# Four products in the first pass over x, its loads cut and queued anew, ten warm-up matmuls for thirteen

## The chip, the cores and the metric

The kernel runs on one core of one Trainium2 chip. The metric is the device time of one execution in microseconds (us); lower is better. The engines named below are TensorE (PE in the profile, its weight loads PEld), VectorE (DVE), ScalarE (ACT), GpSimd (POOL) and SyncE (SP). Loads from HBM are issued by SP, ACT or POOL, each on a queue of its own: q1 is SP's, q10 ACT's, q0 POOL's.

## The reference, cut to what matters

It is one decoder layer over x of 512 tokens by 1024 columns in float32. The change lies in its first step, the gate and up products of the first feed-forward half; everything behind it stays as it is.

```python
x = x + 0.5 * swiglu(rms_norm(x, ffn1_norm), ffn1_gate, ffn1_up, ffn1_down)   # D_FF = 2816
h = rms_norm(x, mix_norm)
...                                   # gated recurrence, short convolution, cross-attention
x = x + 0.5 * swiglu(rms_norm(x, ffn2_norm), ffn2_gate, ffn2_up, ffn2_down)
return rms_norm(x, final_norm)
def swiglu(h, w_gate, w_up, w_down):
    return (jax.nn.silu(h @ w_gate) * (h @ w_up)) @ w_down
```

## The kernel before, in words

x lies transposed on the chip in `xall`: eight tiles k of 128 columns by 512 tokens (256 KB each). A product (m, j) is one block of 128 hidden columns of the gate (j = 0) or up (j = 1) weights: eight weight tiles of 128x128, 64 KB each, against the eight tiles of x, summed in one bank of PSUM. The kernel keeps float32 accuracy by splitting each operand into a high and a low part: `split_x` (lines 123 to 126) gives `x_f1…h` on ACT and `x_f1…l` on DVE, the `split` of `weight_steps` (lines 108 to 111) gives `whi` on ACT and `wlo` on DVE. `mm3` (lines 116 to 121) then makes three matmuls of 512 columns: high by high (L119), high by low (L120), low by high (L121). One product is 24 matmuls.

The order of the first feed-forward half is in `Half.run`. It begins with `first_tile` (lines 472 to 509), which is written by hand: three products, (0,0), (0,1) and (1,0), are made side by side, k by k, so that each tile of x is used three times as it arrives. Its weight pieces come in three cuts (k = 0; 1 and 2; 3 to 7), one unit on each of the three queues, and all of x on SP. Ahead of it thirteen float32 matmuls of 128 columns on a constant tile (line 71, two passes each in the trace) run while nothing has arrived yet. Behind it `run` makes (1,1), then sums the squares of x over the columns on TensorE (`norm.tokens`, `psn_f`), makes (2,0), spreads the row of scales by two matmuls (`norm.rows`, `psb_f`, line 169), and makes (2,1), (3,0) and (3,1). Only with that row (`rsb_f`, called `bc`) can DVE finish any of these products.

Weight units take turns in three buffers each of `raw`, `whi` and `wlo` in `wpool`; a fourth unit waits until the first is split (`raw`) and until its last matmul is done (`whi`, `wlo`). The pool `hp` of the half holds six buffers tagged `raw` and four each of `ah` and `al`, used later: `raw` for seven-product blocks (`Half.load`, lines 293 to 310), `ah` and `al` for the hidden tiles.

The order of instructions on each engine is set at build time by a scheduler from the order of the program and its own costs; at run time each engine takes them strictly in that order. A load issued by ACT stands in ACT's own stream.

Of the kernel before, what the change touches and what calls it, by code (L numbers as in the profile page):

```python
# [8 lines left out]
F32 = mybir.dt.float32  # L9
F32R = mybir.dt.float32r  # L10
# [5 lines left out]
P = 128  # L16
# [4 lines left out]
KT = D // P  # L21
# [17 lines left out]
def decoder_layer(ctx: ExitStack, tc: tile.TileContext, xT, memT, vecs, masks, ident_d,  # L39
                  w1, w1d, w_in, w_i, w_out, w_q, w_k, w_v, w_o, w2, w2d, gfin, out):  # L40
    nc = tc.nc
    const = ctx.enter_context(tc.tile_pool(name="const", bufs=1))
    xpool = ctx.enter_context(tc.tile_pool(name="xpool", bufs=KT))
    wpool = ctx.enter_context(tc.tile_pool(name="wpool", bufs=3))
# [4 lines left out]
    def bank(name):  # L49
        return psp.tile([P, 512], F32, tag="ps", name=name)  # L50

    def r32(ap):
        return ap.bitcast(F32)
# [13 lines left out]
    early = const.tile([P, 1], F32, name="early")  # L67
    nc.scalar.activation(early, mhalf[:, :1], AF.Silu)
    warm = bank("warm")
    for i in range(13):  # L70
        nc.tensor.matmul(warm[:, :P], lhsT=ones, rhs=ones, start=True, stop=True)

    vec = const.tile([P, V_LB], F32, name="vec")
# [6 lines left out]
    xall = xpool.tile([P, KT, S], F32, tag="x", name="xall", bufs=1)  # L80
    x = [xall[:, k] for k in range(KT)]
# [4 lines left out]
    def weights(src, shape):  # L86

        raw, hi, lo, load, split = weight_steps(src, shape)
        load(0, shape[0])
        split(0, shape[0])  # L90
        return hi, lo

    def weight_steps(src, shape):
        n = n_unit[0]
        n_unit[0] += 1
        raw = wpool.tile([P, 1024], F32, tag="raw", name=f"raw{n}")
        hi, lo = (wpool.tile([P, 1024], F32R, tag=t, name=f"{t}{n}") for t in ("whi", "wlo"))
        a, b = shape
        w = a * b

        def load(k0, k1, queue=nc.sync):
            c = slice(k0 * b, k1 * b)
            if len(src.shape) == 3:
                queue.dma_start(raw[:, c].rearrange("p (a b) -> p a b", a=src.shape[1]), src)
            else:
                queue.dma_start(raw[:, c], src[:, c])

        def split(k0, k1):
            c = slice(k0 * b, k1 * b)
            nc.scalar.activation(hi[:, c], raw[:, c], AF.Copy)  # L110
            nc.vector.tensor_tensor(lo[:, c], raw[:, c], r32(hi[:, c]), ALU.subtract)  # L111

        v = lambda t: t[:, :w].rearrange("p (a b) -> p a b", b=b)
        return raw, v(hi), v(lo), load, split

    def mm3(out, wh, wl, xh, xl, first, last):


        nc.tensor.matmul(out, lhsT=wh, rhs=xh, start=first, stop=False)  # L119
        nc.tensor.matmul(out, lhsT=wh, rhs=xl, start=False, stop=False)  # L120
        nc.tensor.matmul(out, lhsT=wl, rhs=xh, start=False, stop=last)  # L121

    def split_x(t, gcol, hi, lo):
        g = vec[:, gcol:gcol + 1]
        nc.scalar.activation(hi, t, AF.Copy, scale=g)
        nc.vector.scalar_tensor_tensor(lo, t, g, r32(hi), op0=ALU.mult, op1=ALU.subtract)
# [47 lines left out]
    def new_split(tag, pool, name, n=S, bufs=KT):  # L174
        return (pool.tile([P, n], F32R, tag=tag + "h", name=name + "h", bufs=bufs),
                pool.tile([P, n], F32R, tag=tag + "l", name=name + "l", bufs=bufs))
# [21 lines left out]
    class Half:  # L198
# [196 lines left out]
        def run(self, first, begin, down, fill, last):  # L395

            p0, p1 = first() if first else ([self.product(0, 0), self.product(0, 1)], [self.product(1, 0)])
            p1.append(self.product(1, 1))  # L400
            self.norm.tokens()
            p2 = [self.product(2, 0)]
            self.bc = self.norm.rows()
            p2.append(self.product(2, 1))
            steps, later = self.inputs_steps()
            self.finish(0, p0)
            self.finish(1, p1)
            steps.pop(0)()
            p3 = [self.product(3, 0), self.product(3, 1)]
            self.finish(2, p2)  # L410
            steps.pop(0)()
            begin(steps + later, lambda: self.finish(3, p3))
            before = None
            for m in range(CLASSIC, FT, 2):
                p1, p5, r6, p2, r7, p4, p3 = self.seven(m)
                p1()
                if before:
                    for s in before:
                        s()
                p5()  # L420
                r6()
                part = [q for q, (a, b) in enumerate(PARTS) if b == m and m > CLASSIC]
                if part:
                    down(part[0])
                p2()
                r7()
                before = p4, p3
            fill()
            for s in before:
                s()  # L430
            last()
# [38 lines left out]
    norm, xs, _ = prepare(V_FFN1, "f1")  # L470

    def first_tile():
        units = [weight_steps(w1[m, j], (KT, P)) for m, j in ((0, 0), (0, 1), (1, 0))]
        ps = [bank(f"ps_f1_{n}") for n in range(3)]
        queues = (nc.sync, nc.scalar, nc.gpsimd)

        def load(k0, k1):
            for u, queue in zip(units, queues):
                u[3](k0, k1, queue)

        nc.sync.dma_start(x[0], xT[:, 0])
        load(0, 1)
        nc.sync.dma_start(x[1], xT[:, 1])
        load(1, 3)
        nc.sync.dma_start(xall[:, 2:4], xT[:, 2:4])
        load(3, 8)
        nc.sync.dma_start(xall[:, 4:6], xT[:, 4:6])
        nc.sync.dma_start(xall[:, 6:8], xT[:, 6:8])
        cuts = [0, 1, 3, 8]
        for k0, k1 in zip(cuts, cuts[1:]):  # L490
            for k in range(k0, k1):
                hi, lo = new_split("x", xpool, f"x_f1{k}")
                split_x(x[k], V_FFN1 + k, hi, lo)
                xs.append((hi, lo))
                if k == k0:
                    for u in units:
                        u[4](k0, k1)
                for j in range(3):
                    mm3(ps[j], units[j][1][:, k], units[j][2][:, k], hi, lo, k == 0, k == KT - 1)
        for k in range(KT):  # L500
            norm.add(x[k])
        nc.scalar.dma_start(ident, ident_d)
        nc.scalar.dma_start(lbv, vecs[:, V_LB:V_LB + 8].rearrange("p (r h) -> p r h", r=2))
        for n in range(0, len(LEVELS), 4):
            e = min(n + 4, len(LEVELS))
            mskf = tmp.tile([P, 4, 2, 64], F32, tag="t2", name=f"mskf{n}")
            nc.scalar.dma_start(mskf[:, :e - n], masks[:, n:e])
            nc.vector.tensor_copy(msk[:, n:e], mskf[:, :e - n])
        return ps[:2], ps[2:]

    norm_m, xs_m, done_m = prepare(V_MIX, "mx")
    with tc.tile_pool(name="hid1", bufs=1, reuse_waits="tile") as hp:
        half = Half("f1", hp, xs, norm, w1, V_FFN1)
# [31 lines left out]
        def last1():  # L545
# [9 lines left out]
            for d in range(4, KT):  # L555
                down_tile(half, "f1", d, len(PARTS) - 1, src1)
                done_m(d)

        half.run(first_tile, begin1, down1, fill1, last1)


    norm_a, xs_a, done_a = prepare(V_XATT, "xa")
    with tc.tile_pool(name="mix", bufs=8, reuse_waits="tile") as mp:
        def big(name):
            return mp.tile([P, NH, S], F32, tag="b", name=name)
# [24 lines left out]
        f = big("f")  # L590
# [7 lines left out]
        for h in range(NH):  # L598
            p = pf[h]
            t = tmp.tile([P, S], F32, tag="t0", name=f"zf{h}")  # L600
# [4 lines left out]
        for h in range(NH):  # L605
            p = project(h)
            t = tmp.tile([P, S], F32, tag="t0", name=f"zq{h}")
# [89 lines left out]
        for hh in range(NH):  # L697
            ps = bank(f"ps_s0_{hh}")
# [14 lines left out]
        for li, h in enumerate(LEVELS):  # L713
# [7 lines left out]
            for half in range(2):  # L721
                ps = bank(f"ps_l{h}_{half}")
# [14 lines left out]
            for r in range(2):  # L737
                qv = qp[:, :, r].rearrange("p g (b u c) -> p g b u c", u=2, c=h)[:, :, :, 1 - r]
                kv = kp[:, :, r].rearrange("p g (b u c) -> p g b u c", u=2, c=h)[:, :, :, r]
                shape = [P, 2 * NH, nb, h]  # L740
# [9 lines left out]
        for half in range(2):  # L750
            ps = bank(f"ps_o1_{half}")
            for n in range(4):
                hh, i = 2 * half + n // 2, 2 * (n % 2)
# [12 lines left out]
        for hh in range(NH):  # L766
            ps = bank(f"ps_o2_{hh}")
# [16 lines left out]
        for i in range(TT):  # L784
            ps = bank(f"ps_o{i}")
# [17 lines left out]
        for hh in range(NH):  # L803
            ps = bank(f"ps_t{hh}")
            for i in range(TT):
                nc.tensor.transpose(ps[:, i * P:(i + 1) * P], on[i][:, hh], ident)
            t = tmp.tile([P, S], F32, tag="t0", name=f"yh{hh}")
            nc.vector.scalar_tensor_tensor(t, ps, vec[:, V_HG + hh:V_HG + hh + 1], sg[:, hh],
                                           op0=ALU.mult, op1=ALU.mult)
            hi, lo = new_split("y", mp, f"yh{hh}")  # L810
# [35 lines left out]
        for m in range(KT):  # L846
# [4 lines left out]
            t = tmp.tile([P, MEM], F32, tag="t0", name=f"km{m}")  # L851
# [129 lines left out]
    with tc.tile_pool(name="hid2", bufs=1, reuse_waits="tile") as hp:  # L981
        half = Half("f2", hp, xs_2, norm_2, w2, V_FFN2)
# [28 lines left out]
        def down(i, j, k, wh, wl):  # L1011
            c = slice(i * P, (i + 1) * P)
            a, b = half.hidden(k)
            p, h, l = po[i][j], wh[:, j], wl[:, j]
            nc.tensor.matmul(p, lhsT=a[:, c], rhs=h, start=k == L0, stop=False)
            nc.tensor.matmul(p, lhsT=a[:, c], rhs=l, start=False, stop=False)
            nc.tensor.matmul(p, lhsT=b[:, c], rhs=h, start=False, stop=k == FT - 1)
# [118 lines left out]
```

## Time and profile before

| what | value |
|---|---|
| median of three runs | 1113.97 us (1113.47 to 1115.74) |
| profiled execution, its own time | 1115.02 us |
| span in its trace, first to last instruction | 1113.2 us |
| PE busy | 1094.7 us (98% of the span) |
| DVE, ACT, POOL busy | 731.2, 485.9, 74.6 us |
| mean granted TensorE clock | 0.995 of full |

The profiled execution took 1.05 us more than the median, and 1.8 us of its time lies outside the span. Times in the rows count from the start of the span.

### The profile page before, as it was taken

The page shows a single profiled execution, that of the slowest core. Times are in us where ns is not written, and L with a number is a line of the kernel's source. Part 1 is how long each engine was busy: PE and PEld are TensorE (multiplying, and loading weights), DVE is VectorE, ACT ScalarE, POOL GpSimd, SP SyncE. Part 2 cuts the span into 40 slices and gives each one's busy share as a digit, 9 for nine tenths or more (in the row PEclk, how much of TensorE's full clock was granted, in tenths as well). Part 3 has the DMA queues.
Part 4 walks back from the last instruction along what each step waited for, and adds up shares of the span by engine and source line. Part 5 has one row for each costly group of instructions (what it writes and reads, how often), then busy time and mean ns, then how long its engine had stood idle before and what let it go on. Part 6 is the DMA issues. An engine that isn't in the chain of part 4 may idle for free. (4 is left out here: it accounts for less than half of the span.)

```text
span 1113.2 us, 15967 instructions
## 1 busy us (share of the span) xinstructions
PE 1094.7 (98%) x6528; PEld 979.4 (88%) x6528; DVE 731.2 (66%) x980; ACT 485.9 (44%) x667; POOL 74.6 (7%) x75
## 2 busy tenths in 40 slices
PE   9989999999999999999999999999989999999997
PEld 7869998998998888888889888888889989989995
DVE  6786755764768566885686556554987747755744
ACT  6435533542545344323364345342545524533553
POOL 0001100110100000000100000000011101100102
PEclk9999999999999999999999999999999999999999
DMA  6467764673523332222244324232287835764521
GB/s 210 127 177 172 195 143 125 164 194 116 160 45 110 97 100 80 81 76 85 67 120 138 122 77 133 74 96 78 84 230 190 186 109 137 203 146 135 114 76 76
DMA packets 68745, 140.53 MB, mean 126 GB/s; under 512 B 4944, under 2 KB 20560, under 8 KB 68672
## 3 DMA queue, kind: packets, MB, share of 16 engines
q1 hardware_dynamic: 54112, 108.02, 30.7%
q0 software_dynamic: 12544, 28.84, 13.2%
q10 hardware_dynamic: 2016, 2.66, 0.7%
q8 instruction: 51, 0.84, 0.3%
q14 instruction: 22, 0.18, 0.1%
HBM read 137.40 MB, written 2.10 MB: 125 GB/s over the span
## 5 line engine op out<-in xcount | busy, mean ns | idle before, releaser
L110 ACT ACTIVATE whi<-raw 128x1024 fp32r<-128x1024 f32 (+4 forms) x143 | 138.0, 970 | 329.5 <-issue 67.4
L111 DVE TENSOR_TENSOR wlo<-raw,whi 128x1024 fp32r<-128x1024 f32 (+4 forms) x143 | 158.6, 1112 | 83.7 <-ACT whi L110 83.1
L316 ACT ACTIVATE whi<-b_f 128x1024 fp32r<-128x1024 f32 x72 | 76.3, 1060 | 104.5 <-issue 34.3
L317 DVE TENSOR_TENSOR wlo<-b_f,whi 128x1024 fp32r<-128x1024 f32 x72 | 88.2, 1225 | 42.3 <-ACT whi L316 40.9
L120 PE MATMUL psd_f<-al_f,whi 128*128 128x512 f32 x280 | 109.1, 390 | 0.0
L121 PE MATMUL psd_f<-ah_f,wlo 128*128 128x512 f32 x280 | 109.1, 390 | 0.0
L119 PE MATMUL psd_f<-ah_f,whi 128*128 128x512 f32 x280 | 108.5, 390 | 0.0
L317 DVE TENSOR_TENSOR wlo<-t_f,whi 128x1024 fp32r<-128x1024 f32 x54 | 66.1, 1224 | 42.6 <-ACT whi L316 42.6
L192 DVE SCALAR_TENSOR_TENSOR xall<-psd_f,xall 128x512 f32<-128x512 f32 x52 | 35.4, 691 | 71.4 <-PE psd_f L121 71.4
L316 ACT ACTIVATE whi<-t_f 128x1024 fp32r<-128x1024 f32 x54 | 57.0, 1056 | 56.6 <-issue 21.3
L121 PEld LDWEIGHTS psd_f<-ah_f,wlo 128*128 128x128 f32 x280 | 52.6, 188 | 10.9
L119 PEld LDWEIGHTS psd_f<-ah_f,whi 128*128 128x128 f32 x280 | 52.6, 188 | 10.8
L120 PEld LDWEIGHTS psd_f<-al_f,whi 128*128 128x128 f32 x280 | 52.6, 188 | 10.7
L338 PE MATMUL psD_f<-q1h_f,whi 128*128 128x256 f32 x144 | 41.2, 286 | 8.3 <-ACT whi L316 8.3
L338 PE MATMUL psA_f<-a11h_f,wlo 128*128 128x256 f32 x144 | 42.2, 293 | 0.0
L338 PE MATMUL psA_f<-a11h_f,whi 128*128 128x256 f32 x144 | 42.1, 292 | 0.0
L338 PE MATMUL psA_f<-a11l_f,whi 128*128 128x256 f32 x144 | 42.1, 292 | 0.0
L338 PE MATMUL psD_f<-q1l_f,whi 128*128 128x256 f32 x144 | 41.0, 284 | 0.0
L338 PE MATMUL psA_f<-a22h_f,whi 128*128 128x256 f32 x144 | 40.9, 284 | 0.0
L338 PE MATMUL psD_f<-q4h_f,wlo 128*128 128x256 f32 x144 | 40.8, 284 | 0.0
L338 PE MATMUL psA_f<-n2h_f,wlo 128*128 128x256 f32 x144 | 40.8, 284 | 0.0
L338 PE MATMUL psA_f<-a22h_f,wlo 128*128 128x256 f32 x144 | 40.8, 284 | 0.0
(778 smaller groups left out, 3209.7 us busy)
## 6 DMA issues: line engine op xcount, KB each, us to landing
b_f<-in_w SPq DMA_DIRECT2D x54, 512.0 KB, 4.0
t_f<-in_w POOLq DMA_DIRECT2D x54, 512.0 KB, 5.7
raw<-in_w_in SPq DMA_DIRECT2D x24, 512.0 KB, 3.5
t_f<-in_w SPq DMA_DIRECT2D x18, 512.0 KB, 5.3
raw<-in_w1d SPq DMA_DIRECT2D x20, 384.0 KB, 3.1
raw<-in_w SPq DMA_DIRECT2D x13, 512.0 KB, 3.5
raw<-in_w2d SPq DMA_DIRECT2D x16, 384.0 KB, 3.1
raw<-in_w2d SPq DMA_DIRECT2D x10, 512.0 KB, 3.4
```

The costliest lines, as they stand in the source:

```text
L110: nc.scalar.activation(hi[:, c], raw[:, c], AF.Copy)
L111: nc.vector.tensor_tensor(lo[:, c], raw[:, c], r32(hi[:, c]), ALU.subtract)
L119: nc.tensor.matmul(out, lhsT=wh, rhs=xh, start=first, stop=False)
L120: nc.tensor.matmul(out, lhsT=wh, rhs=xl, start=False, stop=False)
L121: nc.tensor.matmul(out, lhsT=wl, rhs=xh, start=False, stop=last)
L192: nc.vector.scalar_tensor_tensor(x[k], ps, scale, x[k], op0=ALU.mult, op1=ALU.add)
L316: nc.scalar.activation(hi, raw, AF.Copy)
L317: nc.vector.tensor_tensor(lo, raw, r32(hi), ALU.subtract)
L338: nc.tensor.matmul(o, lhsT=a[:, i, w], rhs=b, start=first and i == 0 and k == 0 and n == 0, stop=k == 3 and n == 2, skip_group_check=True)
```

## The change

Ten warm-up matmuls run in place of thirteen. `first_tile` makes four products, (0,0), (0,1), (1,0) and (1,1); the fourth unit's three tiles are taken from `hp` (one buffer each of `raw`, `ah`, `al`), and `run` no longer makes (1,1) by itself. The cuts are now k = 0; 1; 2 and 3; 4 and 5; 6 and 7. In each cut x comes in two halves of 256 tokens. In the first three cuts SP loads one half of x and unit 0, ACT the other half and unit 1; in the last two SP loads all of these; POOL loads units 2 and 3 throughout. SP and ACT so issue 19 loads on top of `vec` where there were 11, POOL ten where there were three.

```diff
-    for i in range(13):
+    for i in range(10):
         nc.tensor.matmul(warm[:, :P], lhsT=ones, rhs=ones, start=True, stop=True)
...
-            p0, p1 = first() if first else ([self.product(0, 0), self.product(0, 1)], [self.product(1, 0)])
-            p1.append(self.product(1, 1))
+            p0, p1 = first() if first else ([self.product(m, j) for j in range(2)] for m in range(2))
             self.norm.tokens()
...
     def first_tile():
-        units = [weight_steps(w1[m, j], (KT, P)) for m, j in ((0, 0), (0, 1), (1, 0))]
-        ps = [bank(f"ps_f1_{n}") for n in range(3)]
-        queues = (nc.sync, nc.scalar, nc.gpsimd)
-
-        def load(k0, k1):
-            for u, queue in zip(units, queues):
+
+        spare = (half.hp.tile([P, 1024], F32, tag="raw", name="raw_f1x", bufs=6),
+                 half.hp.tile([P, 1024], F32R, tag="ah", name="whi_f1x", bufs=4),
+                 half.hp.tile([P, 1024], F32R, tag="al", name="wlo_f1x", bufs=4))
+        units = [weight_steps(w1[n // 2, n % 2], (KT, P), spare if n == 3 else None) for n in range(4)]
+        ps = [bank(f"ps_f1_{n}") for n in range(4)]
+        cuts = [0, 1, 2, 4, 6, 8]
+        steps = list(zip(cuts, cuts[1:]))
+        for k0, k1 in steps:
+
+            other = nc.scalar if k1 <= 4 else nc.sync
+            for queue, t in ((nc.sync, slice(0, 256)), (other, slice(256, 512))):
+                queue.dma_start(xall[:, k0:k1, t], xT[:, k0:k1, t])
+            for u, queue in zip(units, (nc.sync, other, nc.gpsimd, nc.gpsimd)):
                 u[3](k0, k1, queue)
-
-        nc.sync.dma_start(x[0], xT[:, 0])
-        load(0, 1)
-        nc.sync.dma_start(x[1], xT[:, 1])
-        load(1, 3)
-        nc.sync.dma_start(xall[:, 2:4], xT[:, 2:4])
-        load(3, 8)
-        nc.sync.dma_start(xall[:, 4:6], xT[:, 4:6])
-        nc.sync.dma_start(xall[:, 6:8], xT[:, 6:8])
-        cuts = [0, 1, 3, 8]
-        for k0, k1 in zip(cuts, cuts[1:]):
+        for k0, k1 in steps:
             for k in range(k0, k1):
...
-                for j in range(3):
+                for j in range(4):
                     mm3(ps[j], units[j][1][:, k], units[j][2][:, k], hi, lo, k == 0, k == KT - 1)
```

## Rows read from the trace of the kernel before

**Rows 1.** The page: busy time and share of the span, by engine.
```profile
PE 1094.7 (98%) x6528; PEld 979.4 (88%) x6528; DVE 731.2 (66%) x980; ACT 485.9 (44%) x667; POOL 74.6 (7%) x75
```

**Rows 2.** Timeline, PE, to 38 us: start, duration, line, tile, count, idle before, releaser.
```profile
1.09 5.67 PE L71 MATMUL warm<-ones 128*128 128x128 f32 x26 [1.09 <-DVE mhalf L61]
...
5.52 0.64 PE L71 MATMUL warm<-ones 128*128 128x128 f32 x2
6.37 0.39 PE L71 MATMUL warm<-ones 128*128 128x128 f32 x2
6.51 0.96 PE L119 MATMUL ps_f<-x_f10h,whi 128*128 128x512 f32 x3
8.47 0.39 PE L121 MATMUL ps_f<-x_f10h,wlo 128*128 128x512 f32 x1
9.67 0.50 PE L119 MATMUL ps_f<-x_f11h,whi 128*128 128x512 f32 x1 [0.81 <-ACT whi L110]
14.35 0.39 PE L119 MATMUL ps_f<-x_f13h,whi 128*128 128x512 f32 x1
24.33 0.39 PE L121 MATMUL ps_f<-x_f17h,wlo 128*128 128x512 f32 x1
25.46 0.51 PE L119 MATMUL ps_f<-x_f10h,whi 128*128 128x512 f32 x1 [0.74 <-ACT whi L110]
26.04 0.95 PE L147 MATMUL psn_f<-inv_d,acc_f 128*128 128x1 f32 x8
26.85 0.48 PE L119 MATMUL ps_f<-x_f10h,whi 128*128 128x512 f32 x1
37.38 0.63 PE L169 MATMUL psb_f<-dg_f,ones_r 128*128 128x512 f32 x2
```

**Rows 3.** Windows: length; busy PE, PEld, DVE, ACT, POOL; granted clock; DMA share; GB/s.
```profile
37.38:75.95 38.57, 38.57 (x171) 31.94 (x170) 36.95 (x57) 20.37 (x30) 1.28 (x1) 1.00 0.41 120
75.95:81.37 5.42, 0.40 (x3) 0.19 (x1) 3.00 (x6) 1.06 (x1) 0.77 (x1) 1.00 0.96 236
81.37:85.00 3.63, 3.63 (x17) 3.63 (x18) 2.43 (x2) 1.05 (x1) 1.20 (x1) 0.53 0.57 205
```

**Rows 4.** Timeline of ACT and DVE: first splits; table load; the last diagonal tile.
```profile
4.24 0.72 ACT L125 ACTIVATE x_f10h<-xall,vec 128x512 fp32r<-128x512 f32 x1 [1.56 <-DMA vec<-in_vecs]
4.87 0.49 ACT L110 ACTIVATE whi<-raw 128x128 fp32r<-128x128 f32 x2
6.52 0.31 ACT L110 ACTIVATE whi<-raw 128x128 fp32r<-128x128 f32 x1 [1.16 <-DMA raw<-in_w]
22.96 1.28 ACT L579 ACT_TABLE_LOAD   x1
30.54 0.69 DVE L161 TENSOR_TENSOR dg_f<-ident,rsl_f 128x512 fp32r<-128x512 f32 x1
```

**Rows 5.** Waits of SP's queue, 0 to 60 us: total us, times, longest.
```profile
SPq L488 <- DMA xall<-in_xT: 3.6, 1, 3.6
```

**Rows 6.** DMA issues, 0 to 30 us: count, KB each, median us to landing.
```profile
raw<-in_w POOLq DMA_DIRECT2D x1, 128.0 KB, 6.2
raw<-in_w SPq DMA_DIRECT2D x1, 64.0 KB, 2.9
raw<-in_w ACTq DMA_DIRECT2D x1, 64.0 KB, 3.0
raw<-in_w POOLq DMA_DIRECT2D x1, 64.0 KB, 5.2
```

**Rows 7.** Timeline of POOL: its first three loads (L106).
```profile
1.27 1.86 POOL L106 DMA_DIRECT2D raw<-in_w  x3 [0.83 <-POOLq L1122]
```

**Rows 8.** Waits of SP's queue, 25 to 110 us: total us, times, longest.
```profile
SPq L106 <- DVE wlo L111: 25.2, 4, 9.5
```

**Rows 9.** POOL's queue, 2.5 to 5.5 us, then 5.5 to 8.5: packets, MB, share.
```profile
q0 software_dynamic: 36, 0.09, 16.2%
...
q0 software_dynamic: 104, 0.37, 34.1%
```

More of the change, by code (lines that the diff above doesn't have):

```diff
@@ L91, in weights, with weight_steps @@
         return hi, lo
-    def weight_steps(src, shape):
+    def weight_steps(src, shape, tiles=None):
         n = n_unit[0]
         n_unit[0] += 1
-        raw = wpool.tile([P, 1024], F32, tag="raw", name=f"raw{n}")
-        hi, lo = (wpool.tile([P, 1024], F32R, tag=t, name=f"{t}{n}") for t in ("whi", "wlo"))
+        raw, hi, lo = tiles or (wpool.tile([P, 1024], F32R if t[0] == "w" else F32, tag=t, name=f"{t}{n}")
+                                for t in ("raw", "whi", "wlo"))
         a, b = shape
```

## Prediction, made before the changed kernel ran

> **What bounds the kernel now.** I read the page first: TensorE is busy 98% of the span and no other engine above 66% [rows 1]. So there is little to win but time in which TensorE stands still or runs at half clock, and the change touches only the first forty of 1113 us. Therefore the timeline of PE comes next [rows 2]. The reader is to see its holes. The warm-up passes fill 1.09 to 6.5 us. The first product's first matmuls start at 6.51, but the last one of the first cut starts at 8.47 and the next work at 9.67. The last matmul of the pass starts at 24.33, and only at 25.46 does (1,1) begin. `psb_f`, without which DVE can finish no product, starts at 37.38.
>
> Dense, a matmul of 512 columns takes 0.227 us: 45 of them start from 14.35 to 24.33, 44 steps in 9.98 us [rows 2]. Up to 37.38 TensorE needs 120 of them, 27.24 us, and 0.81 for `psn_f` (26.04 to 26.85). From 6.51 that would end at 34.56, so 2.8 us of holes lie between. With the late start at 6.51 this is all that the change can collect.
>
> What lies behind `psb_f` decides whether it may keep it, so the windows are read next. From 37.38 to 75.95 PE is busy the whole time and DVE 36.95 of 38.57 us; then PE stands for 5.02 us until the weight unit `t1` is there, and the granted clock is 0.53 for the 3.6 us after it [rows 3].
>
> **The warm-ups.** Thirteen make 26 passes, ten make 20. The passes start 0.21 us apart, the 21st at 5.52 [rows 2], so PE is free at 5.52 in place of 6.5. Their clock: two passes from 5.52 on take 0.64 us, two from 6.37 on 0.39 [rows 2]. TensorE thus ran at its lower level (1.2 GHz) nearly to 6.3 us and at 2.4 GHz after. The windows print 1.00 there; the spacing is what I trust. Real matmuls that start before 6.3 are slow: at the lower level 17 matmuls of 256 columns took 3.63 us [rows 3], so I take 0.427 us for one of 512.
>
> **The first cut (k = 0).** The first half product could have begun earlier before, too: `x_f10h` runs from 4.24 to 4.96 and the first two `whi` pieces from 4.87 [rows 4], so the operands of the first matmul are there at about 5.2. Now ACT also issues the other half of x, behind `vec`. An issue costs ACT some 0.4 us, and some of its loads wait: in the trace SP's last x load was held 3.6 us until an earlier x tile had landed [rows 5]. I take 5.7 for the first matmul, with 5.5 and 6.0 as bounds.
>
> There are now twelve matmuls for k = 0. From 5.7 to 6.3 one and a half run slowly, the other ten take 2.3 us: 8.6 if nothing is missing. But two of the four weight pieces come by POOL. A 64 KB piece landed 2.9 us after its issue on SP, 3.0 on ACT and 5.2 on POOL [rows 6], where it was issued at 1.27 [rows 7], so at 6.5. That is why the third `whi` waited until 6.52 [rows 4]. POOL's next 128 KB, issued about 0.6 later, took 6.2, so they landed at 8.0. Unit 3's first 64 KB are half of that: 7.3 by interpolation, and its `whi` is split at 7.6 (0.3 us [rows 4]). If the instruction order keeps all high-by-high matmuls first, as the three of before are at 6.51 [rows 2], nine matmuls stand behind that split: 7.6 + 2.0 = 9.6. If unit 3's come last, 8.6 stays. I take 9.1; landing as late as the 128 KB did (8.0) would make it 10.4.
>
> The Trainium skill (DMA: Bandwidth & Descriptors, Issuing engines are not separate DMA queues) says that loads from all three engines end up on the same 16 DMA engines and interleave there, and that spreading them saves only issue time. This trace differs for small pieces, 5.2 against 2.9 and 3.0 us; by the page unit 3 would not be late, and the cut would end at 8.6.
>
> **The other cuts.** Before, the x tile of k = 1 arrived behind other loads, and the hole from 8.7 to 9.67 came of it. Now its halves are issued ahead of the later cuts, and POOL's pieces for it are 64 KB each. Each k lasts 12 × 0.227 = 2.7 us on PE instead of 2.0, which gives all later cuts more time to arrive: the splits of one k cost ACT about 0.72 + 4 × 0.3 = 1.9 us at most [rows 4]. I count 84 × 0.227 = 19.1 us and 0.2 for short waits on `x_l`, with 0 and 1 as bounds. The pass ends at 9.1 + 19.1 + 0.2 = 28.4.
>
> **Behind the pass.** `psn_f` takes 0.8, (2,0) 24 × 0.227 = 5.45, slow starts 0.1: `psb_f` at 34.7. Before, the hole up to 25.46 came because ACT loaded a table at 22.96 [rows 4] just when it should have split (1,1). Now the unit to be split is (2,0), and nine matmuls of k = 7 and `psn_f` (2.8 us) cover it, as its buffers are released by unit 0, first of four. That is twice the table load (1.28), so it covers that too, or most of it with a split, if it falls there. If the cover fails, the price is about the 0.9 of before. The diagonal tiles for `psb_f` were ready at 31.2 [rows 4], 4.3 after `psn_f`; now 29.2 + 4.3 = 33.5, hidden by (2,0) with 1.2 to spare. The spare tiles of unit 3 shift the turns of `hp` by one: later tiles still wait for the same predecessors, one of them for the spare, free since 28.4. I cost that at nothing; if it failed, the x tiles of the blocks would wait for TensorE.
>
> **The sum.** 37.4 − 34.7 = 2.7 us. Does it last to the end? Up to 75.95 PE runs without a hole, so it keeps the lead. The 5 us wait hangs on a chain of loads on SP, which before that waits for DVE's splits of `wlo` [rows 8], and these for TensorE and for `rsb_f`. Nothing in it goes by absolute time, so I move all of it by 2.7. The profiled execution took 1115.0, 1113.2 of span and 1.8 around it that no edit touches; 1115.0 − 2.7 = 1112.3; against the median, which is 1.05 lower, **1111.3 us**.
>
> **The rivals.**
> *Dense:* unit 3's piece lands with the others and the first cut ends at 8.6, the waits are nil: pass 27.7, `psb_f` 34.0, gain 3.3, 1110.6 us. For it speaks that POOL's pieces are smaller now; against it the 5.2 us for 64 KB.
>
> *Unit 3 stalls the cut:* all high-by-high matmuls first and the landing at 8.0: 1.3 us later than my 9.1, gain 1.4, 1112.6 us. This is a gain too small to be told from none (I take 0.2%, 2.2 us, as the bound).
>
> *Late clock:* PE idles between 5.52 and the first product and again in the first cut; the clock then rises only with k = 1. Twelve matmuls at 0.427 from 5.7 end at 10.8, 1.7 late: gain 1.0, 1113.0 us. For it speaks that before it rose behind warm-up passes without a hole, from 1.09 to 6.3 [rows 2], which now end sooner. The Trainium skill (TensorE: Matmul & The Clock Gate, Part 1, What's actually happening) says that half rate is the default and that activity releases it; the two pass lengths agree with it.
>
> *Given back:* the wait at 81 us does not move along, or another order of instructions later costs as much: 1114.0 us. Against it stand the waits of SP's queue [rows 8].
>
> *Slower:* POOL's queue stays as slow as it was at first. It moved 0.09 MB from 2.5 to 5.5 us and 0.37 in the next three [rows 9]. At 0.03 MB/us the pieces of k = 1 (0.26 MB in all) are through at 11.2 and land about 12.9; PE reaches the end of k = 1 at 15.2, not 11.8, 3.4 late, and the pieces of the third cut are late again. If this holds to about 14 us, another 1.5 is lost there, and the 2.7 turn into a loss of 2.2: 1116.2 us. Below that it isn't slower. Against it: the queue's rate rose fourfold by itself once the first crowd of loads was through.
>
> **How the numbers follow.** Mine (gain 2.0 to 3.1) 0.40, of which 0.30 is above 2.2 us; dense 0.19; unit 3 stalls 0.17; late clock 0.09; given back 0.08; slower 0.07. Faster: 0.30 + 0.19 = 0.49; slower 0.07; the same is the rest, 0.44. The time of the likeliest is 1111.3. The range leaves out the slower rival and most of "given back" above, and gains over 4 us below: 1109.9 to 1113.8. It holds the bounds 5.5 and 8.6 (gain 3.5 with no waits) and 10.4 with 1 us of waits (gain 0.6).
>
> **What the profile will show.** The warm-ups end at 5.5 and the first L119 on `x_f10h` starts before 6.0. The pass holds 96 matmuls, ends near 28.4, and has its largest hole in k = 0 in front of unit 3's matmuls, none before k = 2. No hole of 0.7 us stands before (2,0). `psb_f` starts near 34.7, and the wait before L338 still ends 44 us after `psb_f`, with some 5 us of idle PE. Wrong would be: POOL's first pieces landing behind 8 us, passes or matmuls at half clock beyond 7 us, or a distance from `psb_f` to the end of the span other than the 1075.8 us of before (1113.2 − 37.4).

## Result: slower by 0.42%, and what the profile after shows

The changed kernel takes 1119.5 us (median of 6 runs, 1117.42 to 1121.15) against 1114.84 of the kernel before beside it (6 runs, 1113.47 to 1115.74): ratio 1.0042, 95% interval 1.0028 to 1.0057, so 4.7 us slower where 2.7 less was forecast. Its profiled execution took 1117.42 us, the least of the six, with a span of 1115.6.

The page, busy time and share of the span:
```profile
PE 1093.9 (98%) x6522; PEld 978.7 (88%) x6522; DVE 731.6 (66%) x990; ACT 487.0 (44%) x677; POOL 79.3 (7%) x82
```
But for six warm-up passes TensorE does the same work as in [rows 1], and it is busy 0.8 us less; the span is 2.4 us longer. So the loss is idle time, or matmuls at the lower clock, which count as busy. The timeline of PE says where:
```profile
1.09 4.04 PE L71 MATMUL warm<-ones 128*128 128x128 f32 x20 [1.09 <-DVE mhalf L61]
10.19 1.65 PE L119 MATMUL ps_f<-x_f10h,whi 128*128 128x512 f32 x3 [5.06 <-ACT whi L110]
11.64 0.63 PE L120 MATMUL ps_f<-x_f10l,whi 128*128 128x512 f32 x1
12.07 0.63 PE L121 MATMUL ps_f<-x_f10h,wlo 128*128 128x512 f32 x1
...
14.20 0.58 PE L119 MATMUL ps_f<-x_f10h,whi_f1x 128*128 128x512 f32 x1
14.62 0.39 PE L120 MATMUL ps_f<-x_f10l,whi_f1x 128*128 128x512 f32 x1
...
34.12 0.95 PE L147 MATMUL psn_f<-inv_d,acc_f 128*128 128x1 f32 x8
40.52 0.63 PE L169 MATMUL psb_f<-dg_f,ones_r 128*128 128x512 f32 x2
```
The warm-ups end at 5.13 (forecast 5.5), and then TensorE stands for 5.06 us. The first product starts at 10.19 instead of 6.51 [rows 2], and its matmuls stand 0.43 us apart until 14.6 and 0.23 apart after it: ten of them at 1.2 GHz. `psb_f` comes at 40.52, 3.14 us later than before and 5.8 later than forecast. The windows of that stretch (length; busy PE, PEld, DVE, ACT, POOL; granted clock; DMA share; GB/s) show the same, and that all behind it is dense (a window counts every row that reaches into it):
```profile
5.13:10.19 5.06, 0.00 (x1) 0.00 (x0) 0.21 (x1) 0.97 (x3) 1.74 (x4) 0.76 1.00 318
10.19:14.62 4.43, 4.43 (x11) 3.47 (x11) 3.34 (x11) 3.35 (x12) 0.00 (x0) 0.50 1.06 377
14.62:34.12 19.50, 19.50 (x88) 16.14 (x87) 15.06 (x35) 14.60 (x29) 0.00 (x0) 1.00 0.35 116
```
What is TensorE waiting for? The releaser named is ACT's split, so ACT's timeline is next (the rows to hold against [rows 4]; ACTq is ACT issuing a load):
```profile
0.74 0.41 ACTq L74 DMA_DIRECT2D vec<-in_vecs  x1
...
1.26 0.38 ACTq L484 DMA_DIRECT2D xall<-in_xT  x1
1.67 0.45 ACTq L106 DMA_DIRECT2D raw<-in_w  x1
...
3.02 0.33 ACTq L484 DMA_DIRECT2D xall<-in_xT  x1
5.25 0.34 ACTq L106 DMA_DIRECT2D raw<-in_w  x1
7.69 0.39 ACTq L484 DMA_DIRECT2D xall<-in_xT  x1
8.77 0.34 ACTq L106 DMA_DIRECT2D raw<-in_w  x1
9.22 0.72 ACT L125 ACTIVATE x_f10h<-xall,vec 128x512 fp32r<-128x512 f32 x1 [6.53 <-DMA raw<-in_w]
9.85 0.69 ACT L110 ACTIVATE whi<-raw 128x128 fp32r<-128x128 f32 x3
```
`x_f10h` is split at 9.22, before at 4.24. All six loads of x and weights that ACT makes stand ahead of it in ACT's stream, four of them for k = 1 to 3. Those come at 3.02, 5.25, 7.69 and 8.77, far apart: each waits for an older load. The built program gives the loads of SP and ACT eight semaphores (counters that a load raises when it has landed) in turn, so that each load waits until the one eight before it on the two queues has landed. (With the change SP issues 14 of them and ACT six on top of `vec`, 20 and not 19 as said above.) For ACT's last three these are loads of SP:
```profile
1.65 0.42 SPq L484 DMA_DIRECT2D xall<-in_xT  x1
2.12 0.44 SPq L106 DMA_DIRECT2D raw<-in_w  x1
2.60 0.43 SPq L484 DMA_DIRECT2D xall<-in_xT  x1
```
The DMA issues of these three moments (KB each, us to landing) show half of x for k = 1, unit 0's piece for it and the 256 KB half of the third cut:
```profile
xall<-in_xT SPq DMA_DIRECT2D x1, 128.0 KB, 3.6
raw<-in_w SPq DMA_DIRECT2D x1, 64.0 KB, 5.6
xall<-in_xT SPq DMA_DIRECT2D x1, 256.0 KB, 6.2
```
They so landed at 5.2, 7.7 and 8.8, each just when ACT's waiting load left. All issues to 12 us (medians) show what such pieces took:
```profile
xall<-in_xT SPq DMA_DIRECT2D x5, 256.0 KB, 6.2
raw<-in_w SPq DMA_DIRECT2D x4, 128.0 KB, 5.4
raw_f1x<-in_w POOLq DMA_DIRECT2D x3, 128.0 KB, 5.4
raw<-in_w POOLq DMA_DIRECT2D x3, 128.0 KB, 6.1
...
raw<-in_w ACTq DMA_DIRECT2D x2, 64.0 KB, 5.2
```
The last row is the median of two: ACT's 64 KB for k = 0 took 3.7 us (3.0 in [rows 6]), those for k = 1, which left at 5.25, took 6.6. POOL's timeline holds a second surprise:
```profile
1.28 2.92 POOL L106 DMA_DIRECT2D raw_f1x<-in_w  x5 [0.83 <-POOLq L1119]
4.16 2.16 POOL L106 DMA_DIRECT2D raw<-in_w  x4
```
The loop asks for unit 2 and then unit 3 in each cut; the built order issues all five pieces of unit 3 first. Unit 2's first piece leaves at 4.16, not at 1.3 [rows 7], and the issues of that moment show its landing 5.9 us later, at 10.06:
```profile
raw<-in_w POOLq DMA_DIRECT2D x1, 64.0 KB, 5.9
```

The stall in front of `t1`, to be held against [rows 3]:
```profile
40.52:79.32 38.80, 38.80 (x173) 32.09 (x171) 37.17 (x57) 20.37 (x30) 1.28 (x1) 1.00 0.39 117
79.32:83.05 3.73, 0.17 (x2) 0.00 (x0) 2.77 (x5) 1.06 (x1) 0.77 (x1) 0.97 1.05 260
83.05:86.21 3.16, 3.16 (x15) 3.16 (x16) 2.43 (x2) 0.58 (x1) 1.20 (x1) 0.50 0.92 309
```
TensorE's wait in the second window is 3.56 us long where it was 5.02. It ends at 83.05, 1.68 later than before, so of the 3.14 us it takes back 1.46.

### The profile page after: what moved, and what is told of

It reads as the page before. It is cut to its first block, busy times and chain, and to the rows that moved or that the text cites. A ratio compares the mean times of both kernels' runs of the same rounds, so it can differ in the third digit from the quotient of the medians.

```text
span 1115.6 us, 16009 instructions
## 1 busy us (share of the span) xinstructions
PE 1093.9 (98%) x6522; PEld 978.7 (88%) x6522; DVE 731.6 (66%) x990; ACT 487.0 (44%) x677; POOL 79.3 (7%) x82
## 5 line engine op out<-in xcount | busy, mean ns | idle before, releaser
L110 ACT ACTIVATE whi<-raw 128x1024 fp32r<-128x1024 f32 (+3 forms) x148 | 137.7, 938 | 327.7 <-PE psd_f L120 70.4
L111 DVE TENSOR_TENSOR wlo<-raw,whi 128x1024 fp32r<-128x1024 f32 (+3 forms) x148 | 157.6, 1071 | 81.0 <-ACT whi L110 80.5
L317 DVE TENSOR_TENSOR wlo<-b_f,whi 128x1024 fp32r<-128x1024 f32 x72 | 88.1, 1224 | 42.5 <-ACT whi L316 41.1
L338 PE MATMUL psD_f<-q1h_f,wlo 128*128 128x256 f32 x144 | 40.8, 283 | 0.0
L338 PE MATMUL psA_f<-n2h_f,whi 128*128 128x256 f32 x144 | 40.8, 283 | 0.0
L338 PE MATMUL psA_f<-n2l_f,whi 128*128 128x256 f32 x144 | 40.8, 283 | 0.0
```

The costliest lines, as they stand in the source:

```text
L317: nc.vector.tensor_tensor(lo, raw, r32(hi), ALU.subtract)
L338: nc.tensor.matmul(o, lhsT=a[:, i, w], rhs=b, start=first and i == 0 and k == 0 and n == 0, stop=k == 3 and n == 2, skip_group_check=True)
```

## The experiments

The theory after the two traces had two causes ending within 1 us of each other: ACT's waiting loads (first split at 9.2) and POOL's order (unit 2's first piece at 10.06), with the clock as a consequence of the late start. Each timed version ran beside the kernel before: the first four beside a median of 1116.02 (33 runs), the next four beside 1115.48 (16 runs), the last two beside 1116.00 (21 runs). All read `psb_f` from their own profile; it is 37.38 before and 40.52 changed.

**POOL's loads in the order of the cuts, ACT as changed.**
```diff
-                u[3](k0, k1, queue)
+                behind = tc.issue_after(last) if last and queue is nc.gpsimd else nullcontext()
+                with behind:
+                    r = u[3](k0, k1, queue)
+                last = r.ins if queue is nc.gpsimd else last
```


> POOL's ten loads are issued cut by cut (units 2 and 3 in turn) in place of unit 3's five ahead of unit 2's five; nothing else is changed. If the late start comes from ACT alone (its loads stand ahead of its first split), x_f10h still starts near 9.2 us, the first product near 10.2, and the time is that of the changed kernel, 1119 to 1120. If POOL's order alone did it, the first product starts before 6.5 us and the time falls by about 5 us.

1118.44 us, ratio 1.0021 (1.0011 to 1.0032), `psb_f` 40.87. POOL now alternates between units 2 and 3 from 1.28 on, and `psb_f` comes no earlier:
```profile
8.87 0.72 ACT L125 ACTIVATE x_f10h<-xall,vec 128x512 fp32r<-128x512 f32 x1 [6.18 <-DMA raw<-in_w]
```
ACT's loads alone hold the start to 9.84 us.

**ACT loads only the first cut; the rest of its share goes to SP.** So that the build order cannot put other loads ahead of the first split, the splits of x are tied in their order, those of the weights behind them, and the `ident`, `lbv` and mask loads behind the last split of x. What these ties do by themselves was not measured.
```diff
-            other = nc.scalar if k1 <= 4 else nc.sync
+            other = nc.scalar if k1 <= 1 else nc.sync
...
-                split_x(x[k], V_FFN1 + k, hi, lo)
+                with tc.issue_after(at) if at else nullcontext():
+                    at = split_x(x[k], V_FFN1 + k, hi, lo)
...
```


> ACT issues only the loads of the first cut; the rest of its loads go to SP. POOL's order stays as in the changed kernel. If ACT alone did it, x_f10h starts at 4.2 to 4.8 us, the first product before 6.2, and the time falls by some 5 us to 1114 or less. If POOL's order is a second cause of the same length, two matmuls start before 6.2, then PE stands until the first piece of unit 2 has landed at about 10 us, and the time is within 1 us of the changed kernel's.

1118.09 us, ratio 1.0024 (1.0013 to 1.0035), `psb_f` 39.90. ACT's rows:
```profile
3.98 0.72 ACT L125 ACTIVATE x_f10h<-xall,vec 128x512 fp32r<-128x512 f32 x1 [1.30 <-DMA xall<-in_xT]
4.61 0.29 ACT L110 ACTIVATE whi<-raw 128x128 fp32r<-128x128 f32 x1
6.12 0.31 ACT L110 ACTIVATE whi<-raw 128x128 fp32r<-128x128 f32 x1 [1.22 <-DMA raw<-in_w]
9.79 0.31 ACT L110 ACTIVATE whi<-raw 128x128 fp32r<-128x128 f32 x1 [3.36 <-DMA raw<-in_w]
```
The split of x runs at 3.98 and units 0 and 1 are split by 6.43, but unit 2's first piece, issued by POOL at 4.15, is split only at 9.79. So POOL's order alone holds the cut as long as ACT did. Either cause is enough to keep `psb_f` late. The totals, 2.4 and 2.1 us above the kernel before, may hide a small gain on the changed kernel's 4.7 (4.1 when it ran again, below); the intervals overlap, so that isn't shown.

**Both together.**

> Both edits at once: ACT issues loads of the first cut alone, POOL loads cut by cut. If ACT's waiting loads and POOL's order are the two causes, the first product starts by 6 us, psb_f at 34 to 36 us in place of 40.5, and the time is 1111 to 1114. If instead POOL is too slow for two units, or the smaller loads are, holes of 1 us and more stand in front of k = 1 to 3 and the time stays above 1115.

1114.2 us, ratio 0.999 (0.998 to 0.9999): 1.8 us below the kernel before, hardly clear of noise, and about 4 below the version with either part mended alone. `psb_f` is where it was expected, the time 0.2 us above its range. ACT and PE:
```profile
3.81 0.72 ACT L125 ACTIVATE x_f10h<-xall,vec 128x512 fp32r<-128x512 f32 x1 [1.12 <-DMA xall<-in_xT]
4.44 0.92 ACT L110 ACTIVATE whi<-raw 128x128 fp32r<-128x128 f32 x3
5.66 0.31 ACT L110 ACTIVATE whi_f1x<-raw_f1x 128x128 fp32r<-128x128 f32 x1 [0.30 <-DMA raw_f1x<-in_w]
```
```profile
5.38 1.63 PE L119 MATMUL ps_f<-x_f10h,whi 128*128 128x512 f32 x3
6.80 0.54 PE L120 MATMUL ps_f<-x_f10l,whi 128*128 128x512 f32 x1
7.18 0.39 PE L121 MATMUL ps_f<-x_f10h,wlo 128*128 128x512 f32 x1
...
28.21 0.94 PE L148 MATMUL psn_f<-inv_d,acc_f 128*128 128x1 f32 x8
34.61 0.63 PE L170 MATMUL psb_f<-dg_f,ones_r 128*128 128x512 f32 x2
```
No hole of note in the pass, full clock from about 6.9 us, `psb_f` at 34.61.

**The clock alone: thirty warm-ups in place of ten, all else as changed.**

> Thirty warm-up matmuls in place of ten, so that PE has work until about 10.2 us; all loads as in the changed kernel. If the half clock after the hole costs its share, the first twelve matmuls take 0.23 us each and not 0.43, the pass ends about 2 us earlier, and the time is near 1117.5. If the clock is no part of it, the time stays at 1119.5 (and a first product that still starts at 10.2 us shows that the hole itself hangs on the loads).

1117.88 us, ratio 1.0018 (1.0008 to 1.0028), `psb_f` 38.76:
```profile
1.09 8.73 PE L71 MATMUL warm<-ones 128*128 128x128 f32 x60 [1.09 <-DVE mhalf L61]
10.10 0.49 PE L119 MATMUL ps_f<-x_f10h,whi 128*128 128x512 f32 x1 [0.28 <-ACT whi L110]
```
The product starts as late as in the changed kernel, but its matmuls stand 0.23 us apart from 11.03 on. `psb_f` gains 1.76 us, 0.09 of it by the earlier start: the rest, 1.7, is what the clock cost of the delay, or somewhat more, for the first two matmuls still lose half a microsecond here.

**Ten warm-ups alone, in the kernel before.**

> The kernel before with ten warm-up matmuls; nothing else. PE is free at 5.5 us and the first operands are there at about 5.2, so the first product starts near 5.5; six or seven of its matmuls may run at half clock, and the hole in front of k = 1 grows by what is won. If the shorter warm-up is harmless the time is within 1 us of the kernel before. If it is a cause of the loss (the clock rises later), the time is 2 us or more above it.

1115.6 us, ratio 1.0002 (0.9993 to 1.001), `psb_f` 37.11. The first product starts at 5.38, and k = 1 waits all the same, for x and its weights, until 9.19. The shorter warm-up is worth nothing by itself.

**Four products, with the cuts, queues and warm-ups of before** (in the loop unit 3 follows unit 2 on POOL).
```diff
-        cuts = [0, 1, 2, 4, 6, 8]
+        queues = (nc.sync, nc.scalar, nc.gpsimd, nc.gpsimd)
...
+        cuts = [0, 1, 3, 8]
...
```


> Four products, thirteen warm-ups, but the cuts (0; 1, 2; 3 to 7), the order and the queues of the kernel before, unit 3 on POOL beside unit 2. ACT has only three weight loads, so x_f10h starts at 4.2 to 4.5 us and the first two matmuls by 6.6. POOL issues unit 3's three loads ahead of unit 2's, so the third matmul waits for unit 2's first piece, issued at about 3.2 us: 8.5 to 9.5 us. If that wait is the price of four products, the time lies 0 to 2 us above the kernel before; if the four products themselves cost nothing more, no other hole is seen.

1119.35 us, ratio 1.0036 (1.0022 to 1.0049), `psb_f` 41.52. ACT loads little here; POOL again issues unit 3 first, and the third split waits. The cause is the one expected, but its size was missed: the third matmul starts at 10.99, not 8.5 to 9.5, and the time is 3.9 us above the kernel before, not 0 to 2.
```profile
10.63 0.31 ACT L110 ACTIVATE whi<-raw 128x128 fp32r<-128x128 f32 x1 [5.27 <-DMA raw<-in_w]
```
**The new loads, with three products and thirteen warm-ups.**

> Three products and thirteen warm-ups as before, but the new cuts, halves of x and queues: SP and ACT in the first three cuts, SP alone in the last two, POOL for unit 2 alone. ACT again has six loads, four of them ahead of its first split. If ACT's waiting loads are a cause by themselves, x_f10h starts near 8 to 9 us, the first product a microsecond later at half clock or close to it, and the time is 2 to 5 us above the kernel before. If not, x_f10h starts at 4.2 and the time is that of the kernel before or less.

1119.24 us, ratio 1.0034 (1.0021 to 1.0046), `psb_f` 40.53. POOL has unit 2 alone, issued from 1.27, and ACT's loads do the harm:
```profile
9.66 0.72 ACT L125 ACTIVATE x_f10h<-xall,vec 128x512 fp32r<-128x512 f32 x1 [6.98 <-DMA raw<-in_w]
```
So each half of the change brings one of the two causes, and each half alone costs about what both cost together (3.9 and 3.8 us; the changed kernel beside them, next, 4.1).

**The changed kernel a second time.**

> The changed kernel once more, on the chip of the three runs beside it, for its time there and a second profile. x_f10h should start at 9.0 to 9.4 us again, for it waits for loads and not for the clock; where the clock rises may differ from 14.6 us. If the place of the rise is what spreads the runs, this profile's span differs from 1115.6 by about half of the shift.

1119.55 us, ratio 1.0031 (1.0019 to 1.0043), span 1117.7 in the profile, `psb_f` 40.33. The loss is real. The span is 2.1 us longer than in the first profile, though `psb_f` is no later. The window behind the wait for `t1` shows most of it:
```profile
83.35:89.28 5.93, 5.93 (x28) 5.93 (x28) 3.65 (x3) 1.46 (x2) 2.39 (x2) 0.50 0.97 240
```
Here the granted clock stays at 0.50 for 5.93 us, 28 matmuls, against 3.16 us and 15 in the first profile: 13 more, at 0.213 instead of 0.119 us apart, make 1.2 us.

**Three products with the mended loads** (those of both together; their lines are cut here).
```diff
-            p0, p1 = first() if first else ([self.product(m, j) for j in range(2)] for m in range(2))
+            p0, p1 = first() if first else ([self.product(0, 0), self.product(0, 1)], [self.product(1, 0)])
+            p1.append(self.product(1, 1))
...
```


> The version with ACT's waiting loads moved to SP and POOL's loads put in the order of the cuts, but with three products in the first pass as before (ten warm-ups, (1,1) made after the pass). Theory A (the mending of the loads is all that matters; the fourth product neither costs nor brings much): the first matmul starts near 5.4 us, x and the weight pieces are there for k = 0 and k = 1, and psb_f comes at 34.6 to 35.5, within 1 us of the four products with the same loads; total within 0.1% of theirs and below the kernel before. Rival B (four products per x tile are needed, since three use up a cut in 2.0 us a tile instead of 2.7 and so outrun the loads, and (1,1) starts late): holes of 1 us or more open in front of k = 2 or k = 4 and a hole of about 0.9 us before (1,1); psb_f comes at 36 to 37, total within 0.1% of the kernel before.

1118.15 us, ratio 1.0016 (1.0007 to 1.0026), `psb_f` 38.15. Theory A is refuted. The rival's direction held, and by more than it expected (`psb_f` 38.15 for 36 to 37): three products with these loads are 4.4 us slower than four (1113.77, below). But of its holes only the one in front of (1,1) came; those in front of k = 2 and k = 4 did not, and the one of the pass stands in k = 0. PE:
```profile
6.84 0.73 PE L119 MATMUL ps_f<-x_f10h,whi 128*128 128x512 f32 x2 [1.04 <-ACT whi L110]
...
23.29 0.39 PE L121 MATMUL ps_f<-x_f17h,wlo 128*128 128x512 f32 x1
24.68 0.50 PE L119 MATMUL ps_f<-x_f10h,whi 128*128 128x512 f32 x1 [1.00 <-ACT whi L110]
...
28.05 0.49 PE L121 MATMUL ps_f<-x_f10h,wlo 128*128 128x512 f32 x1 [1.28 <-DVE wlo L111]
```
The pass needs 18.2 us from 5.33 for 72 matmuls (16.3 dense). Behind it stand two more holes that four products cover: ACT's table load at 22.18, as in [rows 4], and DVE's splits of (1,1), which stand behind a cast that waits 2.36 us for the masks. The masks' loads are tied behind the splits by this version's own edit, so part of the second hole comes of that; it was not measured apart.

**Both mended, four products, a second time.**

> The version with both parts of the loading mended and four products, run a second time. If its gain is real, psb_f comes at 34.6 within 0.3 us and the ratio to the kernel before is again 0.998 to 1.000, 3 to 5 us below the changed kernel. If the first result was chance of the clock after the two waits for t1 (there it ran slowly for 15 and 16 matmuls, against 27 and 21 in the second profile of the changed kernel), psb_f is the same, but the total comes out level with the kernel before or above it.

1113.77 us, ratio 0.999 (0.9979 to 1.0), 2.2 us below the kernel before. `psb_f` is 35.43, 0.8 later than in the first run and outside what was expected, because TensorE stood 1.09 us in front of k = 2, until 12.06: ACT had waited 2.74 us for that x tile and split it at 10.98. In the first run the same wait of ACT was 2.69 us and hid behind a first cut that ended later. So the third cut is the next limit of these loads. The total repeats; its interval ends at 1.0.

## Why the prediction was wrong

How far the lead or the delay travels, from the profiles (us; start of a row, or end of the wait):
```
                          before   changed   changed again   both mended
psb_f                      37.38     40.52       40.33          34.61
wait for t1 ends           81.37     83.05       83.35          78.45
first sV_f of ACT          92.40     94.00       95.56          89.47
ACT's q1h_f near 795      795.49    796.88      798.52         792.43
second such wait ends     821.51    824.15      825.26         819.32
span                     1113.2    1115.6      1117.7         1111.0
```

- **What bounds the kernel**: right. TensorE's busy time stayed and the time moved with `psb_f`: later by 3.0 to 3.1, total worse by 4.7 and 4.1; earlier by 2.0 to 2.8, total better by 1.8 and 2.2. The two go together only within some 1.5 us: with POOL's order alone mended `psb_f` was 3.5 later and the total 2.4 worse, with three products and the mended loads 0.8 and 2.2.
- **The warm-ups**: right, and nothing by themselves. They end at 5.13 here and between 4.97 and 5.73 in the other runs with ten, forecast 5.5. What differs is the clock: the passes stand 0.11 us apart from 4.4 us on in the changed kernel, but 0.21 to their end where they end late.
- **The first cut** is the step that failed. The prediction put the first matmul at 5.7 with the sentence "An issue costs ACT some 0.4 us, and some of its loads wait", and sized the waiting at a few tenths. The row it had in hand, 3.6 us of SP's queue held by one x load [rows 5], shows the same kind of wait and most of its price; it was not charged to ACT, where the first split stands behind the loads. Measured: ACT computes nothing for 6.53 us, the first split comes 5.0 us later than before and the first matmul at 10.19, 4.5 later than forecast.
- **Unit 3 late by POOL**, in the same step: POOL does bring a piece too late, but the other one. The prediction let POOL take units 2 and 3 in turn; the built order put unit 3 first, and unit 2's first piece landed at 10.06, beyond the 8.0 that was the worst case for POOL. With POOL in turn and ACT free, unit 3's first piece lands 3.6 and 4.1 us after its issue in the two runs, at 5.6 and 6.1, so its landing, put at 7.3, was over-priced by 1.2 to 1.7 us; unit 2's takes 2.9 and 3.1, so the 5.2 of [rows 6] is not what POOL's queue always takes. The Trainium skill (DMA: Bandwidth & Descriptors, Issuing engines are not separate DMA queues) has it that queues share the engines and spreading saves only issue time. For 128 KB pieces of the changed kernel this agrees (5.4 us on SP, 5.4 and 6.1 on POOL). But the place of an issue in an engine's stream cost 5 us there.
- **Late clock** held as a mechanism, on top of the late start: priced at 1.7 us, it measured 1.7 with thirty warm-ups. That the two agree so well is luck: the price is 2.2 us of slow matmuls less the half of a microsecond that the 9.1 already holds for unit 3, and the run with thirty lost half of one in its first two matmuls. In the changed kernel the twelve matmuls of k = 0 take 4.88 us (10.19 to 15.07) where 2.72 is dense. The prediction took it as one of several ways; it was a consequence of the step that failed.
- **The other cuts and behind the pass**: right here, but the late start gave the loads 4.5 us more than was counted on. From 14.62 TensorE is busy 19.50 of 19.50 us to the end of the pass. With the loads mended, k = 2 waits for its x tile: not at all in the first run, 1.09 us in the second (forecast 0.2, bound 1). From `psn_f` to `psb_f` are 6.40 us (6.35 forecast); no hole stands before (2,0).
- **The sum** comes out where its premise holds: with both causes removed `psb_f` comes at 34.61 and 35.43, forecast 34.7. That the first is within 0.1 us is luck in part: TensorE starts at 5.38, not 5.7, and does not wait for unit 3, but runs its first four matmuls at the lower clock, to about 6.9 us, and the first cut so ends at 9.03 (forecast 9.1). A lead of 2.9 us is there at 92 us and 3.1 at 795.
- **The way to the end** is not as rigid as forecast. From `psb_f` to the end of the wait for `t1` are 43.99 us before, 42.53 and 43.02 changed, 43.84 mended. In the eight profiles with `psb_f` behind 38 us they are 42.5 to 43.0, once 43.8, in the four before it 43.1 to 44.0: a late `psb_f` tends to shorten the wait. Then the clock takes some of it back, by an amount that differs from run to run: from the end of the wait to the first `sV_f` are 10.9 to 11.0 us in seven of the twelve profiles and 11.6 to 12.2 in five. Behind the second such wait the mended version keeps 2.2 of its 3.1 us. From `q1h_f` to the end of that wait are 26.02 us in the profile of before, 26.80 in the run with ten warm-ups alone, whose later order is that of before, and 25.8 to 27.6 in the others. From `psb_f` to the end of the span are 1075.8 us before, as the forecast had it, and 1074.4 to 1077.4 in the others. What makes it vary stays open, and with it the part of the 4.7 us that the 3.1 of `psb_f` leave.
- **Slower** had the right sign for another reason, so its sign was luck. POOL's queue moved 0.14 MB from 2.5 to 5.5 us and 0.38 in the next three, no worse than in [rows 9].

## What to carry to other kernels

A load issued from a computing engine stands in that engine's stream, and if it must wait for an older load, all computing behind it waits too: count what is ahead of the first compute instruction, and put loads of later cuts on a queue that computes nothing. Read the issue order from the built program or the trace, for it need not be that of the loop. Where two causes end at nearly the same time, undoing one shows next to nothing; undo both before judging either.

## What the runs showed of the hardware that was not expected

- After each of the two waits for `t1` TensorE runs at 1.2 GHz (granted clock 0.50), and how long differs between runs of the same kernel: 3.16 and 5.93 us after the first wait in two profiles of the changed kernel. By the spacing of the matmuls this moves the end of the stretch by 1.2 us. The Trainium skill (TensorE: Matmul & The Clock Gate, Part 1, What's actually happening) has idleness bring the lower level and activity release it; the rows agree, and they show that the length is not fixed. In the kernel before, the clock does not fall at once: behind the second wait the first matmuls from 821.51 on still stand 0.12 us apart, and only from 822.24 on 0.21.
- After 5.06 us of idleness behind ten warm-ups the first ten matmuls ran at 1.2 GHz; after 0.28 us behind thirty, all but the first two or three ran at 2.4.
- The time of a 64 KB piece to landing is no constant of its queue: on ACT 3.0 us before [rows 6], 3.7 and 6.6 in the changed kernel; on POOL 5.2 before, 2.9 and 3.1 with both parts mended. More loads at once are a likely reason, which no run shows apart.
